# Splitting loaded weights with one instruction of 1024 columns per engine instead of two of 512, with two buffers per part instead of four

## The chip, the cores and the metric

One core of one Trainium2 chip runs the kernel. The metric is device time in microseconds, from the program's start to its end; the shown times are medians of several executions.

## What is computed

One step of a hybrid decoder layer, in float32, for 320 tokens: a prompt of 256 and 8 sequences of 8. The same weights serve all tokens.

```python
proj = rms_norm(x, ln1_g) @ w_in          # 2048 -> 7440 columns
o_a, ... = gdn_mixer(proj[..., :4112])    # gated delta rule, 8 heads of 128
o_b, ... = rwkv_mixer(proj[..., 4112:])   # RWKV-7, 16 heads of 64
x = x + concat([o_a, o_b]) @ w_o          # 2048 x 2048
f, ... = conv_ffn(rms_norm(x, ln2_g))     # w_up 2048 x 11264, conv, silu gate, w_down 5632 x 2048
y = rms_norm(x + f, final_g)              # and the new states of both mixers and the convolutions
```

## The kernel before

Every big product runs as a stream of weights past tokens that stay in SBUF. Weights come from DRAM in pieces of up to 1024 columns (8 tiles of 128x128, 512 KB) into three `raw` buffers of [128, 1024]. To keep float32 accuracy with the fast fp32r matmul, each weight W is split into whi, W rounded to fp32r, and wlo = W - whi. The tokens are split in the same way into xh and xl. For each weight tile, TensorE then does three matmuls of 128x128 by 128x320: whi with xh, whi with xl, and wlo with xh. In a trace, `mm`, `rA`, `rB` and `g` are PSUM tiles that take such sums, and `h`, `fx`, `b`, `bi` hold split tokens.

The split is done in halves. `wpieces` (line 534) cuts all weights into pieces (`self.raws`) and each piece into two parts (`self.halves`): 1024 columns become 512 and 512, and the last piece of a down-projection output, 768 columns, becomes 384 and 384. Three threads feed the stream:

- `wload` (line 553) takes a raw buffer and issues the load on the SyncE queue (line 507).
- `whi` (line 560) takes a buffer of `hi_s` and copies one half with ScalarE (line 438).
- `wlo` (line 567) takes a buffer of `lo_s` and subtracts with VectorE (line 461). When the last half of a piece is done, it frees the raw buffer.

`stream` (line 579) issues the matmuls (line 409) and, when a half has been used up, frees its buffer of `hi_s` and of `lo_s`. Both pools hold four buffers of [128, 512] (lines 670 and 671).

The order of all instructions is made by a planner while the program is built. Work is written as threads that yield operations. `run` (line 339) keeps a modelled clock for each engine and gives out the next operation by readiness and by priority, where a lower number goes first. Each engine then executes its list strictly in that order, so an instruction that waits holds up all behind it on its engine. The stream has priority 1000 on TensorE, and matmuls of the mixers go ahead of it; the mixers' threads have 10 and more, the evacuation of PSUM has 2. A split has priority 1 when it is urgent and 500 otherwise:

```python
urgent = lambda: 1 if self.nsplit - self.np < CFG["ug"] else 500   # line 692; ug is 1
```

Here `nsplit` is the number of the last part whose wlo was given out and `np` the number of the part that the stream is using.

The stages follow each other in one stream: w_ab and w_in (117 pieces, with the mixers' own small operations beside them; `xt`, `bi`, `c`, `s`, `st` are tiles of theirs, and the solve of a triangular system runs on `xt`), w_o in three parts a, b and c (32 pieces), then twice half of w_up (88 pieces) and half of w_down (48 pieces). In part c of w_o each of 16 outputs is half a piece; VectorE adds the sum to x and makes the low part of the next stage's tokens, and GpSimd sums squares (`ssa`).

Of the kernel before, what the change touches and what calls it, by code (L numbers as in the profile page):

```python
# [26 lines left out]
RC = 5  # L27
# [66 lines left out]

CFG = dict(es=0, eg=1, ln=1, bl=0, re=(7,), rg=1, gp={3: 5}, nw=(3, 4), b5=4, b4=4, b2=6, c2=9, b1=12, bi=8, raw=7, xt=2, ord='R0 R1 G0 R2 R3 Z0 G1 R4 R5 Z1 G2 R6 R7 Z2 G3 Z3', dl=1900, wr=2, l2=300, ra=3, war=1, vt=150, lw=1, lh=2, s1=9, st=6, m=60, ev=80, sp=0, cv=0, pq=1000, ug=1, sg=0, gv=1023, fs=105, pl=3000, pd=1000, pr=0.4605, ch=100, gs=1.0, hw=3400, ha=0.42, vg=350, pq2=0, lk=1, mv=126, oc=0, qn=0, aw=1.0, ls=1500, lr=600, lg=1500, hv=114, hs=125, lx=0, l3=3, hp=0, ab=0)

# [71 lines left out]
class Prog:  # L170
# [363 lines left out]
    def wpieces(self, units):  # L534
        self.halves, self.raws = [], []
        for ap, ncol, m in units:
            step = max(m, 1024 // m * m)
            n = -(-ncol // step)
            k = ncol // m
            per = -(-k // n) * m  # L540
            at = 0
            while at < ncol:
                w = min(per, ncol - at)
                self.raws.append((ap[:, at:at + w], w))
                mid = -(-w // m // 2) * m
                for o, z in ((0, mid), (mid, w - mid)):
                    if z:
                        self.halves.append((len(self.raws) - 1, o, z, m, o + z == w))
                at += w
        self.raw, self.hi, self.hl = {}, {}, {}  # L550
        self.nsplit = self.np = self.pk = 0
# [73 lines left out]
    def build(self):  # L625
        tc, a = self.tc, self.a
# [4 lines left out]
        wp = left.enter_context(tc.tile_pool(name="wp", bufs=1))  # L631
        hp = left.enter_context(tc.tile_pool(name="hp", bufs=1))
# [12 lines left out]
        for x in CFG["ord"].split():  # L645
            n = int(x[1:])
# [20 lines left out]
        self.wpieces(units)  # L667
        self.pool_q = [q for q in range(15, 400) if q % CFG["pq"] == CFG["pq"] - 1 and self.halves[q][0] < 2 * 59 + 1]
        self.raw_s = Slots(self, wp, "raw", [P, 1024], CFG["nw"][0])
        self.hi_s = Slots(self, wp, "whi", [P, 512], CFG["nw"][1], F32R)  # L670
        self.lo_s = Slots(self, wp, "wlo", [P, 512], CFG["nw"][1], F32R)
        self.hslots = Slots(self, hp, "h", [P, NTOK], 32, F32R)
        self.gps = PSlots(self, self.ps, "g", [P, 512], 2)
        self.rA = PSlots(self, self.ps, "rA", [P, 512], 2)
# [28 lines left out]
    def start(self):  # L703

        a, V, G, KT = self.a, self.V, self.G, self.KT
        yield self.ms(G, self.ones, 1.0)
        yield self.ms(G, self.eps1, 1e-6)
        if CFG["lk"]:
            yield self.ms(G, self.zero, 0.0)
        yield self.dma(self.vec[:, 0:48], a["vec"][:, 0:48])  # L710
        self.rs = self.b1.take()
        self.h, self.hr, self.hw = {}, {}, {}
        big = [(self.b5, 4)] * 4 + [(self.b4, 3)] * 4 + [(self.b1, 1)] * 4
# [41 lines left out]
        g = yield from self.take(self.gps, 1)  # L755
# [364 lines left out]
    def rwkv(self, i, box):  # L1120
        V, G = self.V, self.G
        b1, b2, b5, gps, s1 = self.b1, self.b2, self.b5, self.gps, self.s1
# [107 lines left out]
        for c0, n in ((0, 2), (2, 2), (4, 1)):  # L1230
            yield from self.want(gps)
            g = gps.take()
            for c in range(n):
                for h in range(2):
                    o = g[:, 256 * c:256 * c + 256].rearrange("p (x h t) -> p x h t", x=2, h=2)[:, :, h]
                    yield self.mm(o, kbc[:, c0 + c], ar[:, c0 + c, :, h])
            m = self.c("rmask" if c0 < 4 else "rmasks")
            m = m.rearrange("p (x t) -> p x t", x=2)
            yield self.tt(V, at[:, c0:c0 + n], g[:, 0:256 * n].rearrange("p (c x t) -> p c x t", c=n, x=2),
                    m.unsqueeze(1).to_broadcast([P, n, 2, P]), ALU.mult)  # L1240
            gps.give()
        scr = self.drams([NS, 1024], f"scr{i}")
        scx = self.drams([8, GG, NS, 32], f"scx{i}")
        sv = scr.rearrange("(f m) (s t) -> f s m t", f=2, t=32)
# [46 lines left out]
            sqd.append(c)  # L1291
        e = G if i in CFG["re"] else V
        st = {"left": 2, "held": ((self.st, dec), (b5, ar_, at_), (b2, kt_, vu_, xd_))}
        sample = self.rwkv_sample(i, st, at, ar, kt, vu, vu_, xd_, xh, yv, dec, sm)
        if CFG["es"] == 2:
            self.spawn(sample, self.cur.prio + CFG["sp"])
        yield from self.solve(mt_, xt_, tm_)
# [146 lines left out]
                    m[:, j:j + 1, j + 1:32].to_broadcast([np_, q, w]), ALU.mult)  # L1444
            yield self.tt(V, x[:, 0:q, j + 1:32], x[:, 0:q, j + 1:32], t, ALU.subtract)

    def rwkv_sample(self, i, st, at, ar, kt, vu, vu_, xd_, xh, yv, dec, sm):
        V, G = self.V, self.G
        ident = self.c("ident")[0:64, 0:64]
        yield from self.want(self.b4)  # L1450
        w_ = self.b4.take()
        ss = w_[:, 0:512].rearrange("p (b x) -> p b x", b=NB)
        yield self.dma(ss, self.a["srw"][i], lag=CFG["ls"])
        yield self.ms(G, w_[64:128, 512:768], 0.0)
# [23 lines left out]
        yield from self.want(self.b4)
        vm_ = self.b4.take()
        vm = vm_[:, :].rearrange("p (h b x) -> p h b x", h=2, b=NB)  # L1480
        for h in range(2):
            yield self.tt((self.g(4), V)[h], vm[:, h], vu[:, 4, h:h + 1].to_broadcast([P, NB, 64]),
                    self.c("bm").unsqueeze(2).to_broadcast([P, NB, 64]), ALU.mult)
# [4 lines left out]
        yield from self.want(self.rB)
        pb = self.rB.take()
        for h in range(2):  # L1490
            yield self.mm(pb[64 * h:64 * h + 64], kt[:, 4, 64 * h:64 * h + 64], vm_[:, 512 * h:512 * h + 512])
        yield self.tt(V, w_[:, 0:512], w_[:, 0:512], pb, ALU.add)
        self.rB.give()
# [401 lines left out]
    def gdn_sample(self, p, st, kq, kw, vn, xd, qkd, ob, ssk, hd):  # L1895
        V, G = self.V, self.G
        gs, b4, s1 = self.gs, self.b4, self.s1
        yield from self.want(b4, 4 if CFG["eg"] == 0 else 3)
        ss = [b4.take(), b4.take()]
        rp_ = b4.take()  # L1900
        kr, rr = (rp_[:, o:o + 512].bitcast(F32R).rearrange("p (g x) -> p g x", g=4) for o in (0, 512))
# [11 lines left out]
        yield from self.want(s1, 1)  # L1913
        hi = s1.take()[:, :].bitcast(F32R)
        yield from self.triple(kr, kw[:, 4], hi, 1)
        yield from self.want(self.rA, 1, s1, 2)
        pa = self.rA.take()
        rt, qs = s1.take(), s1.take()
# [8 lines left out]
        yield lambda: "x" in st  # L1927
        yield self.mm(pa[:, 256:384], xd[:, 4], rt)
        yield self.pcp(rt, pa[:, 256:384], 4)
        yield self.mm(pa[:, 384:512], qkd[:, 4], rt)  # L1930
        yield self.tt(V, ob[:, 4], pa[:, 384:512], qs, ALU.add)
        self.spawn(self.gdn_square(ob, ssk, 4, hd), self.cur.prio)
        self.rA.give()
        if not CFG["gv"] & 1:
            for h in range(2):
                yield self.tt(G, sv[h], sv[h], gs["gls"][:, p, h].unsqueeze(2).to_broadcast([P, NB, P]), ALU.mult)
        yield from self.triple(rr, rt, hi, 0)
        s1.give(3)
        kr = rp_[:, 0:512].bitcast(F32R).rearrange("p (h q x) -> p h q x", h=2, q=2)
# [141 lines left out]
```

## Time and profile before

| what | value |
|---|---|
| median of 3 runs | 1716.24 us (1713.74 to 1716.97) |
| the profiled execution | 1717.03 us, span 1715.2 us |
| TensorE busy | 1677.3 us, 98% of the span |
| VectorE busy | 1239.8 us, 72% |
| ScalarE busy | 1021.7 us, 60% |
| GpSimd busy | 178.7 us, 10% |
| moved by DMA | 256.53 MB, mean 150 GB/s |

The span goes from the first to the last instruction; the execution's time has some 1.8 us more. In the profile PE is TensorE's matmul, PEld its weight load, DVE is VectorE, ACT ScalarE, POOL GpSimd. L409 is line 409. A row of a timeline merges equal instructions that follow each other ("x2") and ends with the idle time of the engine before them, and what ended it.

### The profile page before, as it was taken

To read this page: it belongs to the slowest core of one execution; us is meant where nothing else is said; L and a number is where in the kernel's file an instruction comes from. 1 tells how busy PE (TensorE), PEld (TensorE's weight loads), DVE (VectorE), ACT (ScalarE), POOL (GpSimd) and SP (SyncE) were. 2 spreads that over 40 slices of the span, in tenths; PEclk is the share of its full clock that TensorE was granted. 3 is DMA by queue.
4 is the path that set the end of the run, shared out by engine and by line. 5 is a ranking of instruction groups with operands and counts; after the bars stand their busy time and mean duration, and the time that the engine had idled before them with its cause. 6 is when DMAs were issued, how large, how long until landed. Compare 5 with 4: busy or idle time off the path is not lost.

```text
span 1715.2 us, 33329 instructions
## 1 busy us (share of the span) xinstructions
PE 1677.3 (98%) x11959; PEld 1623.2 (95%) x11959; DVE 1239.8 (72%) x3351; ACT 1021.7 (60%) x2394; POOL 178.7 (10%) x482
## 2 busy tenths in 40 slices
PE   8999999999999989999999999999999999999997
PEld 7998999889988989899999999999999999999996
DVE  8989889879998987787666666544466666665443
ACT  7886877688678856666555544433345545545442
POOL 0200000000000000231111111000011111110101
PEclk9999999999999999999999999999999999999998
DMA  6444534435353556455444444555444444444544
GB/s 231 130 133 127 170 119 141 124 122 163 114 165 100 171 167 190 138 170 163 153 150 149 148 149 151 147 153 148 152 153 151 151 148 148 150 152 144 154 145 148
DMA packets 102967, 256.53 MB, mean 150 GB/s; under 512 B 31953, under 2 KB 41425, under 8 KB 102801
## 3 DMA queue, kind: packets, MB, share of 16 engines
q1 hardware_dynamic: 102080, 253.09, 47.2%
q8 instruction: 94, 1.54, 0.4%
q10 hardware_dynamic: 720, 1.31, 0.2%
q14 instruction: 73, 0.59, 0.1%
HBM read 239.14 MB, written 15.22 MB: 148 GB/s over the span
## 4 chain that ended last, share of the span: by engine, by line
PE 79%; DVE 7%; DMA 4%; ACT 3%; issue 1%; POOL 0%; SPq 0%; DVEq 0%; ACTq 0%; POOLq 0%
PE mm L409 32%; PE rA L409 22%; PE rB L409 20%; PE g L409 5%; DVE wlo L461 2%; DMA b<-scr 2%; DVE xt L461 1%; ACT b L438 1%; DMA b<-scx 1%; DVE bi L456 1%; DVE b L461 1%; PE g L421 1%; ACT whi L438 0%; ACT L438 0%; DVE h L456 0%
## 5 line engine op out<-in xcount | busy, mean ns | idle before, releaser
L438 ACT ACTIVATE whi<-raw 128x512 fp32r<-128x512 f32 (+2 forms) x842 | 519.6, 621 | 543.2 <-PE mm L409 185.7
L461 DVE TENSOR_TENSOR wlo<-raw,whi 128x512 fp32r<-128x512 f32 (+2 forms) x842 | 573.8, 682 | 336.4 <-ACT whi L438 331.8
L409 PE MATMUL mm<-h,whi 128*128 128x320 f32 x2992 | 689.7, 314 | 0.2 <-DVE h L461 0.2
L409 PEld LDWEIGHTS mm<-h,whi 128*128 128x128 f32 x2992 | 504.3, 189 | 4.1 <-issue 2.2
L409 PE MATMUL mm<-h,wlo 128*128 128x320 f32 x1496 | 470.4, 314 | 0.3 <-DVE wlo L461 0.3
L409 PEld LDWEIGHTS mm<-h,wlo 128*128 128x128 f32 x1496 | 282.2, 189 | 3.6 <-issue 1.3
L409 PE MATMUL rB<-h,whi 128*128 128x320 f32 x1136 | 250.6, 309 | 0.0
L409 PE MATMUL rA<-h,whi 128*128 128x320 f32 x1136 | 250.6, 309 | 0.0
L409 PEld LDWEIGHTS rB<-h,whi 128*128 128x128 f32 x1136 | 189.8, 188 | 0.1
L409 PEld LDWEIGHTS rA<-h,whi 128*128 128x128 f32 x1136 | 189.8, 188 | 0.0
L409 PE MATMUL rB<-h,wlo 128*128 128x320 f32 x568 | 175.6, 309 | 0.3 <-DVE wlo L461 0.3
L409 PE MATMUL rA<-h,wlo 128*128 128x320 f32 x568 | 175.3, 309 | 0.0
L474 POOL COPY sfo<-f 128x18 f32<-128x18 f32 x88 | 61.8, 703 | 690.3 <-DVE f L461 690.3
L409 PEld LDWEIGHTS rB<-h,wlo 128*128 128x128 f32 x568 | 106.5, 188 | 0.7 <-DVE wlo L461 0.6
L409 PEld LDWEIGHTS rA<-h,wlo 128*128 128x128 f32 x568 | 106.5, 188 | 0.0
L456 DVE SCALAR_TENSOR_TENSOR f<-f,vec,f 128x336 f32<-128x336 f32 x176 | 102.9, 584 | 3.6 <-ACT f L438 0.3
L461 DVE TENSOR_TENSOR b<-b,b 80x54 f32<-80x54 f32 (+27 forms) x295 | 76.7, 261 | 9.7 <-ACT b L438 7.0
L409 PE MATMUL rA<-fx,whi 128*128 128x320 f32 x336 | 74.1, 309 | 0.0
L409 PE MATMUL rB<-fx,whi 128*128 128x320 f32 x336 | 74.1, 309 | 0.0
L409 PE MATMUL rA<-b,b 128*32 128x128 f32 (+3 forms) x488 | 55.2, 283 | 2.9 <-DMA b<-srw 2.9
L438 ACT ACTIVATE f<-f,vec 128x336 f32<-128x336 f32 x88 | 50.8, 577 | 10.3 <-DVE f L461 1.5
L409 PEld LDWEIGHTS rA<-fx,whi 128*128 128x128 f32 x336 | 56.1, 188 | 0.0
(261 smaller groups left out, 2356.0 us busy)
## 6 DMA issues: line engine op xcount, KB each, us to landing
raw<-w_up SPq DMA_DIRECT2D x176, 512.0 KB, 3.5
raw<-w_in SPq DMA_DIRECT2D x116, 512.0 KB, 4.0
raw<-w_dn SPq DMA_DIRECT2D x64, 512.0 KB, 3.6
raw<-w_dn SPq DMA_DIRECT2D x32, 384.0 KB, 3.1
raw<-w_oa SPq DMA_DIRECT2D x16, 512.0 KB, 3.9
b<-sgdn SPq DMA_DIRECT2D x8, 512.0 KB, 4.4
o_sgs<-b SPq DMA_DIRECT2D x8, 512.0 KB
raw<-w_ob SPq DMA_DIRECT2D x8, 512.0 KB, 5.2
```

The costliest lines, as they stand in the source:

```text
L409: op = Op("T", cost, (out,), (lhsT, rhs), lambda: self.nc.tensor.matmul(out, lhsT, rhs, start=start, stop=stop))
L421: op = Op("T", (1, 0.836 * self.width(in_), 107), (out,), (in_,), lambda: self.nc.tensor.transpose(out, in_, ident))
L438: lambda: self.nc.scalar.activation(out, in_, func, **kw), {AF.Exp: "E", AF.Ln: "L", AF.Silu: "S", AF.Tanh: "T"}.get(func))
L456: lambda: self.V.scalar_tensor_tensor(out, in0, scalar, in1, op0=op0, op1=op1)))
L461: lambda: e.tensor_tensor(out, in0, in1, op=op)))
L474: return self.shared(Op(self.key(e), v if e is self.V else CFG["gs"] * (120 + 3.33 * n), (out,), (in_,), lambda: e.tensor_copy(out, in_)))
```

## The change

One instruction per engine splits a whole piece. The part that `wpieces` cuts becomes as wide as the piece, so that the second part is empty; the buffers of whi and wlo become [128, 1024], two of each. They take the same space as four of [128, 512]. The diff has further options (`seg`, `ss`, `lz`, `rt`, `pv`, `bw`), among them other ways to compute a part of the mixers; their values keep the old code in use.

```diff
-CFG = dict(es=0, eg=1, ... nw=(3, 4), ... hp=0, ab=0)
+CFG = dict(es=0, eg=1, ... nw=(3, 4), ... hp=0, ab=0, seg=(), ss=0, lz=1000, wf=1, rt=0, pv=0, wn=2, bw=0)
...
     def run(self):
+        turns = list(CFG["seg"])
         while self.threads:
+            while turns and self.clk["T"] >= 1e3 * turns[0][0]:
+                CFG.update(turns.pop(0)[1])
...
                 self.raws.append((ap[:, at:at + w], w))
-                mid = -(-w // m // 2) * m
+                mid = w if CFG["wf"] else -(-w // m // 2) * m
                 for o, z in ((0, mid), (mid, w - mid)):
                     if z:
                         self.halves.append((len(self.raws) - 1, o, z, m, o + z == w))
...
         self.raw_s = Slots(self, wp, "raw", [P, 1024], CFG["nw"][0])
-        self.hi_s = Slots(self, wp, "whi", [P, 512], CFG["nw"][1], F32R)
-        self.lo_s = Slots(self, wp, "wlo", [P, 512], CFG["nw"][1], F32R)
+        ww, wn = (1024, CFG["wn"]) if CFG["wf"] else (512, CFG["nw"][1])
+        self.hi_s = Slots(self, wp, "whi", [P, ww], wn, F32R)
+        self.lo_s = Slots(self, wp, "wlo", [P, ww], wn, F32R)
```

## Rows read from the trace of the kernel before

**Rows 1.** The page, engines: busy us (share of the span) xinstructions

```profile
PE 1677.3 (98%) x11959; PEld 1623.2 (95%) x11959; DVE 1239.8 (72%) x3351; ACT 1021.7 (60%) x2394; POOL 178.7 (10%) x482
```

**Rows 2.** Table of stretches: start:end, length, busy us by engine, clock, DMA

```profile
60.00:600.00 540.00, 529.14 (x4044) 492.81 (x4043) 480.50 (x1747) 425.68 (x1255) 46.76 (x129) 1.00 0.44 137
...
600.00:760.00 160.00, 152.20 (x1155) 141.59 (x1154) 123.39 (x395) 94.81 (x272) 21.24 (x51) 0.98 0.58 172
...
800.00:1700.00 900.00, 900.00 (x6139) 899.84 (x6138) 546.40 (x1026) 425.66 (x724) 91.95 (x269) 1.00 0.48 149
```

**Rows 3.** TensorE's waits: who waited for whom, us in total, times, longest us

```profile
PE mm L409 <- ACT b L438: 5.6, 2, 5.5
...
PE rA L409 <- DMA b<-srw: 2.9, 1, 2.9
...
PE mm L409 <- DVE wlo L461: 0.3, 1, 0.3
```

**Rows 4.** Groups by form: operation, tiles, shape, count, busy us, mean ns, idle

```profile
L438 ACT ACTIVATE whi<-raw 128x512 fp32r<-128x512 f32 x776 | 485.5, 630 | 485.6 <-PE mm L409 171.3 <-PE rB L409 129.1 <-PE rA L409 117.8
...
L438 ACT ACTIVATE whi<-raw 128x384 fp32r<-128x384 f32 x64 | 33.6, 525 | 56.6 <-PE rB L409 22.7 <-PE rA L409 19.4 <-PE mm L409 14.4
...
L461 DVE TENSOR_TENSOR wlo<-raw,whi 128x512 fp32r<-128x512 f32 x776 | 537.5, 694 | 267.8 <-ACT whi L438 263.2 <-DMA o_srp<-s 0.8
...
L461 DVE TENSOR_TENSOR wlo<-raw,whi 128x384 fp32r<-128x384 f32 x64 | 35.8, 559 | 65.3 <-ACT whi L438 65.3
```

**Rows 5.** Timeline of 900 to 912 us: start, duration, engine, operation, [idle before]

```profile
906.34 0.31 PE L409 MATMUL mm<-h,wlo 128*128 128x320 f32 x1
...
906.60 0.63 ACT L438 ACTIVATE whi<-raw 128x512 fp32r<-128x512 f32 x1 [1.14 <-PE mm L409]
...
907.27 0.69 DVE L461 TENSOR_TENSOR wlo<-raw,whi 128x512 fp32r<-128x512 f32 x1
...
907.95 1.21 DVE L456 SCALAR_TENSOR_TENSOR f<-f,vec,f 128x336 f32<-128x336 f32 x2
...
910.16 0.19 PEld L409 LDWEIGHTS mm<-h,wlo 128*128 128x128 f32 x1
...
907.34 0.58 ACT L438 ACTIVATE f<-f,vec 128x336 f32<-128x336 f32 x1
```

**Rows 6.** Chain that ended last: start, us, what, number of instructions

```profile
1121.34 19.35 PE mm L409 x132
```

**Rows 7.** Timeline of VectorE and GpSimd, 747 to 756 us

```profile
753.60 0.54 DVE L456 SCALAR_TENSOR_TENSOR h<-h,vec,h 128x320 fp32r<-128x320 f32 x1
...
754.06 0.47 DVE L461 TENSOR_TENSOR h<-h,mm 128x320 f32<-128x320 f32 x1
...
754.46 0.97 DVE L461 TENSOR_TENSOR wlo<-raw,whi 128x512 fp32r<-128x512 f32 x1
...
755.36 0.54 DVE L456 SCALAR_TENSOR_TENSOR h<-h,vec,h 128x320 fp32r<-128x320 f32 x1
...
753.88 1.01 POOL L461 TENSOR_TENSOR ssa<-ssa,f 128x320 f32<-128x320 f32 x1 [0.75 <-ACT f L438]
```

**Rows 8.** Timeline of ScalarE, VectorE and TensorE, 128 to 138 us

```profile
129.28 1.15 ACT L438 ACTIVATE whi<-raw 128x512 fp32r<-128x512 f32 x2 [0.32 <-DMA raw<-w_in]
...
134.17 0.68 DVE L461 TENSOR_TENSOR wlo<-raw,whi 128x512 fp32r<-128x512 f32 x1
...
134.77 0.22 DVE L461 TENSOR_TENSOR xt<-xt,b 80x66 f32<-80x66 f32 x1
...
137.23 0.57 PE L421 MATMUL g<-cst,bi 128*128 128x128 f32 x3 [1.07 <-DVE bi L456]
```

**Rows 9.** Group of wlo in the stretch of 60 to 760 us

```profile
L461 DVE TENSOR_TENSOR wlo<-raw,whi 128x512 fp32r<-128x512 f32 x266 | 183.0, 690 | 24.1 <-ACT whi L438 22.4 <-DMA o_srp<-s 0.8
```

**Rows 10.** Table of stretches of 5 us, two with a lowered clock

```profile
330.00:335.00 5.00, 5.00 (x27) 4.87 (x26) 3.02 (x13) 3.84 (x11) 0.00 (x0) 0.66 0.67 228
...
625.00:630.00 5.00, 5.00 (x23) 5.00 (x23) 3.20 (x18) 2.15 (x10) 0.00 (x0) 0.50 0.13 12
```

More of the change, by code (lines that the diff above doesn't have):

```diff
@@ L91 @@
 WO = {"a": (8, 9, 10, 11, 12, 13, 0, 1), "b": (2, 3, 4, 5), "c": (14, 15, 6, 7)}
-CFG = dict(es=0, eg=1, ln=1, bl=0, re=(7,), rg=1, gp={3: 5}, nw=(3, 4), b5=4, b4=4, b2=6, c2=9, b1=12, bi=8, raw=7, xt=2, ord='R0 R1 G0 R2 R3 Z0 G1 R4 R5 Z1 G2 R6 R7 Z2 G3 Z3', dl=1900, wr=2, l2=300, ra=3, war=1, vt=150, lw=1, lh=2, s1=9, st=6, m=60, ev=80, sp=0, cv=0, pq=1000, ug=1, sg=0, gv=1023, fs=105, pl=3000, pd=1000, pr=0.4605, ch=100, gs=1.0, hw=3400, ha=0.42, vg=350, pq2=0, lk=1, mv=126, oc=0, qn=0, aw=1.0, ls=1500, lr=600, lg=1500, hv=114, hs=125, lx=0, l3=3, hp=0, ab=0)
+CFG = dict(es=0, eg=1, ln=1, bl=0, re=(7,), rg=1, gp={3: 5}, nw=(3, 4), b5=4, b4=4, b2=6, c2=9, b1=12, bi=8, raw=7, xt=2, ord='R0 R1 G0 R2 R3 Z0 G1 R4 R5 Z1 G2 R6 R7 Z2 G3 Z3', dl=1900, wr=2, l2=300, ra=3, war=1, vt=150, lw=1, lh=2, s1=9, st=6, m=60, ev=80, sp=0, cv=0, pq=1000, ug=1, sg=0, gv=1023, fs=105, pl=3000, pd=1000, pr=0.4605, ch=100, gs=1.0, hw=3400, ha=0.42, vg=350, pq2=0, lk=1, mv=126, oc=0, qn=0, aw=1.0, ls=1500, lr=600, lg=1500, hv=114, hs=125, lx=0, l3=3, hp=0, ab=0, seg=(), ss=0, lz=1000, wf=1, rt=0, pv=0, wn=2, bw=0)
 LAT = {"VV": 127, "AA": 143, "GG": 102, "TT": 0, "VT": CFG["vt"], "AT": CFG["vt"] + 15, "GT": CFG["vt"] + 30, "TV": 196, "TA": 268, "TG": 200,
@@ L709, in start @@
             yield self.ms(G, self.zero, 0.0)
-        yield self.dma(self.vec[:, 0:48], a["vec"][:, 0:48])
+        yield self.dma(self.vec[:, 0:48], a["vec"][:, 0:48], self.A if CFG["pv"] else None)
         self.rs = self.b1.take()
@@ L1229, in rwkv @@
         kbc = kb_[:, :].rearrange("p (c x) -> p c x", c=RC)
[L1230 to L1233, printed above, removed]
-                for h in range(2):
[L1235 to L1241, printed above, removed]
+        if CFG["rt"]:
+            for c0, n in ((0, 4), (4, 1)):
+                yield from self.want(gps, 2)
+                two_ = (gps.take(), gps.take())
+                for c in range(n):
+                    for h in range(2):
+                        z = slice(64 * h, 64 * h + 64)
+                        yield self.mm(two_[h][:, 128 * c:128 * c + 128].rearrange("p (x t) -> p x t", x=2), kb[z, c0 + c].rearrange("p x t -> p (x t)"), ar[z, c0 + c, :, h])
+                m = self.c("rmask" if c0 < 4 else "rmasks")
+                m = m.rearrange("p (x h t) -> p h x t", x=2, h=2)
+                for h in range(2):
+                    yield self.tt(V, at_[:, :].rearrange("p (x c h t) -> p h c x t", c=RC, x=2, h=2)[:, h, c0:c0 + n], two_[h][:, 0:128 * n].rearrange("p (c x t) -> p c x t", c=n, x=2),
+                            m[:, h].unsqueeze(1).to_broadcast([P, n, 2, 64]), ALU.mult)
+                gps.give(2)
+        else:
+            for c0, n in ((0, 2), (2, 2), (4, 1)):
+                yield from self.want(gps)
+                g = gps.take()
+                for c in range(n):
+                    for h in range(2):
+                        o = g[:, 256 * c:256 * c + 256].rearrange("p (x h t) -> p x h t", x=2, h=2)[:, :, h]
+                        yield self.mm(o, kbc[:, c0 + c], ar[:, c0 + c, :, h])
+                m = self.c("rmask" if c0 < 4 else "rmasks")
+                m = m.rearrange("p (x t) -> p x t", x=2)
+                yield self.tt(V, at[:, c0:c0 + n], g[:, 0:256 * n].rearrange("p (c x t) -> p c x t", c=n, x=2),
+                        m.unsqueeze(1).to_broadcast([P, n, 2, P]), ALU.mult)
+                gps.give()
@@ L1293, in rwkv @@
         st = {"left": 2, "held": ((self.st, dec), (b5, ar_, at_), (b2, kt_, vu_, xd_))}
-        sample = self.rwkv_sample(i, st, at, ar, kt, vu, vu_, xd_, xh, yv, dec, sm)
+        sample = self.rwkv_sample(i, st, at, ar, kt_, kt, vu, vu_, xd_, xh, yv, dec, sm)
         if CFG["es"] == 2:
@@ L1445, in solve, with rwkv_sample @@
             yield self.tt(V, x[:, 0:q, j + 1:32], x[:, 0:q, j + 1:32], t, ALU.subtract)
-    def rwkv_sample(self, i, st, at, ar, kt, vu, vu_, xd_, xh, yv, dec, sm):
+    def rwkv_sample(self, i, st, at, ar, kt_, kt, vu, vu_, xd_, xh, yv, dec, sm):
         V, G = self.V, self.G
         ident = self.c("ident")[0:64, 0:64]
-        yield from self.want(self.b4)
+        yield from self.want(self.b4, 1 + CFG["bw"])
         w_ = self.b4.take()
+        vm_ = self.b4.take() if CFG["bw"] else None
         ss = w_[:, 0:512].rearrange("p (b x) -> p b x", b=NB)
@@ L1477, in rwkv_sample @@
         self.s1.give(rr)
[L1478 to L1483, printed above, removed]
+        if CFG["ss"] & 1:
+            scs = self.drams([P, 2, P], f"scs{i}")
+            for n, z in enumerate((kt_, vu_)):
+                yield self.dma(scs[:, n], z[:, 512:640], self.q)
         yield self.mm(pa[:, 384:512], at[:, 4, 1], vu_[:, 512:640], start=False)
@@ L1487, in rwkv_sample @@
         self.rA.give()
[L1488 to L1493, printed above, removed]
+        if not CFG["bw"]:
+            yield from self.want(self.b4)
+            vm_ = self.b4.take()
+        if CFG["ss"] & 1:
+            sr = scs.rearrange("(x q s t) w c -> x s t q (w c)", x=2, q=2, s=4)
+            for x in range(4):
+                for n in range(2):
+                    o = 32 * x + 8 * n
+                    yield self.dma(vm_[o:o + 8, 0:512].rearrange("p (q y) -> p q y", q=2), sr[n, x], self.q, lag=CFG["lz"])
+        else:
+            vm = vm_[:, :].rearrange("p (h b x) -> p h b x", h=2, b=NB)
+            for h in range(2):
+                yield self.tt((self.g(4), V)[h], vm[:, h], vu[:, 4, h:h + 1].to_broadcast([P, NB, 64]),
+                        self.c("bm").unsqueeze(2).to_broadcast([P, NB, 64]), ALU.mult)
+        if CFG["ss"] & 1:
+            for x in (0, 2):
+                yield from self.want(self.rA, 1, self.rB)
+                two = (self.rA.take(), self.rB.take())
+                for q in range(2):
+                    for h in range(2):
+                        for y in range(2):
+                            z, o = vm_[32 * (x + y):32 * (x + y) + 16], 256 * q + 64 * h
+                            yield self.mm(two[y][64 * h:64 * h + 64, 64 * q:64 * q + 64], z[:, o:o + 64], z[:, o + 128:o + 192])
+                for y in range(2):
+                    sb = ss.rearrange("p (q s) x -> p s q x", q=2)[:, x + y]
+                    yield self.tt(V, sb, sb, two[y][:, 0:128].rearrange("p (q x) -> p q x", q=2), ALU.add)
+                self.rA.give()
+                self.rB.give()
+        else:
+            yield from self.want(self.rB)
+            pb = self.rB.take()
+            for h in range(2):
+                yield self.mm(pb[64 * h:64 * h + 64], kt[:, 4, 64 * h:64 * h + 64], vm_[:, 512 * h:512 * h + 512])
+            yield self.tt(V, w_[:, 0:512], w_[:, 0:512], pb, ALU.add)
+            self.rB.give()
         self.b4.give(vm_)
@@ L1897, in gdn_sample @@
         gs, b4, s1 = self.gs, self.b4, self.s1
-        yield from self.want(b4, 4 if CFG["eg"] == 0 else 3)
+        strips = CFG["ss"] & 2
+        yield from self.want(b4, 4 if CFG["eg"] == 0 else 2 if strips else 3)
         ss = [b4.take(), b4.take()]
-        rp_ = b4.take()
-        kr, rr = (rp_[:, o:o + 512].bitcast(F32R).rearrange("p (g x) -> p g x", g=4) for o in (0, 512))
+        if not strips:
+            rp_ = b4.take()
+            kr, rr = (rp_[:, o:o + 512].bitcast(F32R).rearrange("p (g x) -> p g x", g=4) for o in (0, 512))
         sv = [t[:, :].rearrange("p (b x) -> p b x", b=NB) for t in ss]
@@ L1912, in gdn_sample @@
                 yield self.cp((V, G)[x], dst, kq[h][:, 4, x].rearrange("p (g j t) -> p g j t", g=2, t=8))
-        yield from self.want(s1, 1)
-        hi = s1.take()[:, :].bitcast(F32R)
-        yield from self.triple(kr, kw[:, 4], hi, 1)
+        if not strips:
+            yield from self.want(s1, 1)
+            hi = s1.take()[:, :].bitcast(F32R)
+            yield from self.triple(kr, kw[:, 4], hi, 1)
+        else:
+            scs = self.drams([P, 2, P], f"gscs{p}")
+            sr = scs.rearrange("(a s t) w c -> s t a (w c)", a=4, s=4)
+            yield self.dma(scs[:, 0], kw[:, 4], self.q)
         yield from self.want(self.rA, 1, s1, 2)
@@ L1929, in gdn_sample @@
         yield self.pcp(rt, pa[:, 256:384], 4)
+        if strips:
+            yield self.dma(scs[:, 1], rt, self.q)
         yield self.mm(pa[:, 384:512], qkd[:, 4], rt)
@@ L1936, in gdn_sample @@
                 yield self.tt(G, sv[h], sv[h], gs["gls"][:, p, h].unsqueeze(2).to_broadcast([P, NB, P]), ALU.mult)
+        if strips:
+            s1.give(2)
+            b4.give(km_)
+            yield from self.want(b4)
+            z_ = b4.take()
+            for x in range(4):
+                yield self.dma(z_[32 * x:32 * x + 8, :].rearrange("p (a y) -> p a y", a=4), sr[x], self.q, lag=CFG["lz"])
+            for x in (0, 2):
+                yield from self.want(self.rA, 1, self.rB)
+                pb = (self.rA.take(), self.rB.take())
+                for a in range(4):
+                    for y in range(2):
+                        z = z_[32 * (x + y):32 * (x + y) + 8, 256 * a:256 * a + 256]
+                        yield self.mm(pb[y][:, 128 * a:128 * a + 128], z[:, 0:128], z[:, 128:256])
+                for a in range(4):
+                    for y in range(2):
+                        h, b = a // 2, 4 * (a % 2) + x + y
+                        yield self.stt(sv[h][:, b], sv[h][:, b], gs["gls"][:, p, h, b:b + 1], pb[y][:, 128 * a:128 * a + 128])
+                self.rA.give()
+                self.rB.give()
+            for h in range(2):
+                yield self.dma(self.a["o_sgs"][2 * p + h], sv[h])
+            b4.give(3)
+            self.release(st)
+            return
         yield from self.triple(rr, rt, hi, 0)
```

## The prediction

> **What bounds the kernel now.** The page's engine table comes first: TensorE is busy 1677.3 us, 98% of the span [rows 1]. A mean over stages hides which of them waits, so the table of stretches is next [rows 2]. From 800 to 1700 us (the feed-forward part) TensorE is busy 900.00 of 900 us, with VectorE at 546.40 and ScalarE at 425.66. Nothing but its own matmuls bounds it there; no saving elsewhere can shorten these 900 us, only a new wait can lengthen them. From 60 to 760 us (the mixers) TensorE is idle 10.9 + 7.8 = 18.7 us, while VectorE is busy 480.5 of 540 and then 123.4 of 160: TensorE and VectorE are both nearly full. Third view: what TensorE waits for [rows 3]. Its longest waits end on ScalarE's and a DMA's chain work for the mixers; on the split weights (wlo) it waits 0.3 us in all by that row. So today the split costs TensorE nothing, and the question is whether that stays so with half as many, larger instructions and buffers.
>
> **How much reserve the split has now.** A matmul of 320 columns follows the one before in 19.35/132 = 0.1466 us [rows 6]; a half piece (4 key tiles, 3 matmuls each) lasts 1.76 us on TensorE, a whole one 3.52 us. In the feed-forward part one half goes like this [rows 5]: its buffer's last matmul starts at 906.34, ScalarE starts whi at 906.60 (0.26 later) for 0.63, VectorE starts wlo at 907.27 (0.04 after ScalarE's end) for 0.69. The half is ready 0.26 + 0.63 + 0.04 + 0.69 = 1.62 us after that matmul. With four buffers three halves lie ahead: 36 matmuls, 5.28 us. The first matmul to read wlo is the third of its half, 0.44 us after the last matmul of the half before, and its weight load stands 0.14 ahead, so the due time is 5.28 + 0.30 = 5.58. Reserve: 3.96 us.
>
> **The change, step by step.** Of the new options in the diff only wf=1 and wn=2 do anything; the others are off.
>
> *The instructions.* The trace has no split of 1024 columns. The 384- and 512-column forms give the slope [rows 4]: ScalarE 525 and 630 ns, so 1024 columns take 630 + 4 x 105 = 1.05 us; VectorE 559 and 694 ns, so 694 + 4 x 135 = 1.23 us. Upper ends are two of the old (1.26 and 1.39 us: no saving). An end below the slope would need columns to become cheaper with width, which these rows give no reason for. I take 1.05 and 1.23. What is saved per piece is less than the difference of durations, because instructions that follow each other overlap: two whi together take 1.15 us, 0.52 from start to start, and after a wlo of 0.68 the next VectorE instruction starts at 134.77, 0.60 after 134.17 [rows 8]. On a full VectorE the saving is 2 x 0.60 - (0.60 + 0.54) = 0.06 us a piece; apart from other work it is 2 x 0.694 - 1.23 = 0.16. From 60 to 760 us 266 halves, 133 pieces, are split [rows 9]: 8 to 21 us of VectorE's 604.
>
> *The buffers, feed-forward part.* A buffer is freed when a whole piece has been used, and its successor is due after one other piece. Ready: 0.26 + 1.05 + 0.04 + 1.23 = 2.58 us (2.95 at the upper ends). Due: 3.52 + 0.30 = 3.82 (the load at 910.16 less the matmul at 906.34 [rows 5]). The reserve falls from 3.96 to 1.24 us (0.87). What can stand in front: on ScalarE one instruction of up to 0.58, on VectorE one of the pair of 1.21 us [rows 5], some 0.6; together 1.2, just covered. The planner also helps: a split is urgent (priority 1) when no piece lies ready beyond the one in use, and with two buffers that is so every time one comes free. I cost the 900 us at zero. If the cover goes, each 0.1 us a piece costs 26 us (900/3.52 = 256 pieces).
>
> *Down projection.* Each output has pieces of 1024, 1024 and 768 columns. The first piece of an output is split while the 768 one (18 matmuls, 2.64 us) runs: due at 2.94, ready at 2.58 (2.95), reserve 0.36 (zero). VectorE's add for the output before comes at another turn, when the 768 piece ends and the due time is again 3.82. Zero, with an upper end of 32 outputs x 0.5 = 16 us if an add (0.48 us [rows 7]) gets in front.
>
> *Output projection's last part.* Here VectorE is exactly full: per half an add (0.40 from start to start), a wlo of 0.97 that GpSimd's sum (1.01 us beside it) stretches from 0.69 (0.90 to the next), and a multiply of 0.46: 1.76 us, the 1.76 of TensorE [rows 7]. For a whole piece after: 2 x 0.86 + 1.14 + two stretches of 0.28 = 3.42 of 3.52. It fits, but ready comes at 2.58 + 0.56 and with one instruction in front at 3.7, against 3.82. Eight pieces: 0 to 4 us; I take 1.
>
> *Mixers.* Four effects. (a) VectorE gets its 8 to 21 us back. (b) A link of a mixer's chain that meets a split waits behind 1.23 in place of 0.69 us; with the saving this about cancels in the queue. (c) Splits now go first whenever a buffer is free, where they used to give way until the next half was missing. (d) The reserve is smaller: an engine held up in its own order by more than 1.24 us now stops the stream, where 3.96 was covered. TensorE's idle there is not for weights: at 137.23 it waits 1.07 us for a VectorE chain result [rows 8], while the wlo of 134.17 had been done for over a microsecond; stream matmuls stand behind the late one in TensorE's order. So (a) can win only part of the 18.7 us: -2 us, ends -9 and 0. (c) and (d): +1, ends 0 and +15. The DMA side moves little: a raw buffer is freed when the whole piece is split, 2.58 in place of 1.62 us after the release, with two further raw pieces (7 us of TensorE) loaded by then.
>
> *Clock.* TensorE ran at the lower of its two levels (1.2 in place of 2.4 GHz) for part of two stretches of the mixers, after it had stood idle: 0.66 granted in 330 to 335 and 0.50 in 625 to 630 us [rows 10]: by these two rows 1.7 + 2.5 = 4.2 us. Another order may lose one or gain one: 0, plus or minus 2.
>
> **Sum.** 0 + 0 + 1 - 2 + 1 + 0 = 0. The profiled execution took 1717.03 us, 1.8 of it outside the span of 1715.2, and lies 0.8 above the median of 1716.24. Forecast for the median: 1716.
>
> **A rule against it.** The rows show ScalarE and VectorE far from full from 800 us on and TensorE without a gap [rows 2]. The Trainium skill (Perfetto Trace Analysis, Optimizing Scalar/DVE Operations) says that larger operations pay where the engine is saturated, and that where these engines are not saturated but make others wait, instructions should be broken up. By that rule the change pays at most in the mixers and is a risk in the long stage; the trace agrees so far that there is no gap there to make worse. It stands as the fifth rival below.
>
> **The rivals.**
> 1. Faster: VectorE's queue decides the mixers' idle time. For: they are 89% and 77% full there and waits end on their chain work. Against: most of the idle time is latency. Half of 18.7 us less 2 us for 1: -8, so 1708 (1702 to 1712).
> 2. Slower: the stream stops in the mixers, effects (c) and (d), in 60 to 800 us. From 3.4/149 = 0.02 us a piece on average it is seen; a stop of 0.4 us at one piece in six costs 149/6 x 0.4 = 10, so 1726 (1720 to 1735).
> 3. Slower by the down projection's tight turn: 4 to 16 us, 1720 to 1732, say 1726.
> 4. No saving at all (two of the old per instruction, 1.26 and 1.39): reserve 0.87, still 1716 to 1719.
> 5. A regular gap in the long stage, if both instructions of the 1.21 pair and 0.58 on ScalarE stand in front: 1.79 - 1.24 = 0.55 on one piece of each of 88 outputs: 48 us, 1764.
>
> **How the numbers follow.** A measurement of this kernel can tell about 0.2%, 3.4 us. Chances: forecast 0.36 (own range 1713 to 1719), rival 1 0.31, rival 2 0.20, rival 3 0.06, rival 4 0.03, rival 5 0.04. Faster 0.31; same 0.36 + 0.03 = 0.39; slower 0.30. The range goes from 1706 (about a quarter of rival 1 below) to 1730 (rival 5 and the tails of 2 and 3 above): 0.18 left out.
>
> **What will show it.** Right: splits of 1.05 and 1.23 us; TensorE 900 of 900 from 800 us on, no idle time ended by wlo; the difference, if any, before 800 us. Wrong: waits of TensorE on wlo or whi above 3 us in all (rivals 2, 3, 5; their place tells which), TensorE's idle time in 60 to 760 below 12 us (rival 1), stretches of the mixers at the lower clock other in number than two.

## The result and the profile after

The changed kernel takes 1726.88 us (median of 8 runs, 1724.10 to 1735.16), the kernel before 1717.23 us beside it (8 runs). The ratio is 1.0063, with a 95% interval of 1.0050 to 1.0075: slower by about 10 us. The profiled execution has a span of 1723.7 us, 8.5 more than before.

First the table of stretches of the changed kernel: start:end and length, busy us of TensorE, its weight loads, VectorE, ScalarE and GpSimd (with counts), granted clock, DMA share, GB/s.

```profile
0.00:60.00 60.00, 51.79 (x336) 45.95 (x337) 50.94 (x105) 43.37 (x78) 3.11 (x9) 1.00 0.63 209
60.00:600.00 540.00, 526.02 (x4005) 487.54 (x4004) 474.36 (x1601) 405.82 (x1142) 42.24 (x122) 1.00 0.44 135
600.00:760.00 160.00, 149.26 (x1140) 138.13 (x1139) 123.12 (x396) 86.96 (x239) 18.43 (x53) 0.98 0.54 160
760.00:800.00 40.00, 40.00 (x273) 39.84 (x272) 31.85 (x49) 29.67 (x48) 16.09 (x22) 1.00 0.51 170
800.00:1700.00 900.00, 900.00 (x6140) 900.00 (x6139) 509.47 (x768) 357.67 (x464) 54.71 (x271) 1.00 0.48 150
```

Held against [rows 2]: from 800 us on TensorE is again busy 900.00 of 900 us, although VectorE and ScalarE have less to do. In the mixers its idle time grows from 10.86 to 540 - 526.02 = 13.98 us and from 7.8 to 10.74. So the loss lies wholly ahead of 800 us. Next comes the split itself, in the groups by form (operation, tiles, shape, count, busy us, mean ns):

```profile
L464 DVE TENSOR_TENSOR wlo<-raw,whi 128x1024 fp32r<-128x1024 f32 x388 | 475.2, 1225 | 258.1 <-ACT whi L441 257.2
L441 ACT ACTIVATE whi<-raw 128x1024 fp32r<-128x1024 f32 x388 | 409.8, 1056 | 493.4 <-issue 275.6 <-PE mm L412 102.0 <-PE rB L412 49.0
```

What was worked out from [rows 4] as 1.23 and 1.05 us is measured as 1.225 and 1.056. One turn of the feed-forward part, in the timelines of the engines (start, duration, engine, operation, idle time before):

```profile
900.70 0.31 PE L412 MATMUL rA<-h,wlo 128*128 128x320 f32 x1
...
900.95 1.06 ACT L441 ACTIVATE whi<-raw 128x1024 fp32r<-128x1024 f32 x1 [2.10 <-issue]
...
902.04 1.23 DVE L464 TENSOR_TENSOR wlo<-raw,whi 128x1024 fp32r<-128x1024 f32 x1 [0.44 <-ACT whi L441]
...
904.52 0.19 PEld L412 LDWEIGHTS rB<-h,wlo 128*128 128x128 f32 x1
```

The buffer's last matmul starts at 900.70, the new piece is ready at 902.04 + 1.23 = 903.27, 2.57 us later; it is due with the weight load at 904.52, 3.82 us later. The reserve is 1.25 us; [rows 5] had led to 1.24.

In the mixers TensorE waits on a split twice, and one of the two stops is its longest there (who waited for whom, us in total, times, longest):

```profile
PE g L412 <- DVE wlo L464: 4.2, 1, 4.2
PE mm L412 <- DVE wlo L464: 1.5, 1, 1.5
```

The longest stands near 628 us. The timelines of VectorE, TensorE and SyncE's queue there:

```profile
622.45 1.21 DVE L464 TENSOR_TENSOR wlo<-raw,whi 128x1024 fp32r<-128x1024 f32 x1
628.80 0.49 DVE L464 TENSOR_TENSOR h<-h,mm 128x320 f32<-128x320 f32 x1 [5.15 <-DMA h<-xT]
...
631.45 1.21 DVE L464 TENSOR_TENSOR wlo<-raw,whi 128x1024 fp32r<-128x1024 f32 x1
...
632.72 0.42 PE L412 MATMUL g<-h,wlo 128*128 128x320 f32 x1 [4.24 <-DVE wlo L464]
...
621.74 0.65 SPq L510 DMA_DIRECT2D b<-gscr  x1
622.48 0.40 SPq L510 DMA_DIRECT2D h<-xT  x1
```

VectorE stands 5.15 us before an add that needs a load; the next wlo is behind that add in VectorE's order, and TensorE, which needs it, stops for 4.24 us. In the kernel before a hold-up of VectorE of similar length, here behind ScalarE, cost almost nothing. Its timeline of VectorE has

```profile
101.06 0.55 DVE L456 SCALAR_TENSOR_TENSOR b<-bi,vec,b 128x320 f32<-128x320 f32 x1 [4.28 <-ACT b L438]
```

TensorE's only gap beside it is one of 0.18 us that ended on another result. So the first theory was this: **theory 1**, the smaller reserve lets hold-ups through. The rivals are **theory 2**, splits that always go first delay the mixers' chains, and **theory 3**, any new order of the instructions gives another time, by chance. A fourth, **theory 4**, came with the experiments: the wide instruction itself delays the chains.

**A part of the diff that the prediction missed.** With `bw=0` the new code is not the old one. In `rwkv_sample` the two masked products of the sample tokens now come after the matmul and the row sums of the output, and were ahead of them:

```diff
-        yield from self.want(self.b4)
-        vm_ = self.b4.take()
-        vm = vm_[:, :].rearrange("p (h b x) -> p h b x", h=2, b=NB)
-        for h in range(2):
-            yield self.tt((self.g(4), V)[h], vm[:, h], ...)
         yield self.mm(pa[:, 384:512], at[:, 4, 1], vu_[:, 512:640], start=False)
         yield from self.rows(yv[:, 4], pa, 384, sm[:, 4:5])
...
+        if not CFG["bw"]:
+            yield from self.want(self.b4)
+            vm_ = self.b4.take()
...
+            for h in range(2):
+                yield self.tt((self.g(4), V)[h], vm[:, h], ...)
```

The work is the same, its place in the mixers is not. All kernels of the experiments were made from the changed source, with `wf=0` where the text says "old split" or an expectation says "the kernel before": they hold this move too, and the kernel before alone is without it. Comparisons among them are not touched by it. Every ratio to the kernel before contains it, the result's own too, and no run isolates it.

### The profile page after: what moved, and what is told of

It reads as the page before. It is cut to its first block, busy times and chain, and to the rows that moved or that the text cites. A ratio compares the mean times of both kernels' runs of the same rounds, so it can differ in the third digit from the quotient of the medians.

```text
span 1723.7 us, 31955 instructions
## 1 busy us (share of the span) xinstructions
PE 1678.8 (97%) x11959; PEld 1622.3 (94%) x11959; DVE 1198.2 (70%) x2930; ACT 927.7 (54%) x1973; POOL 139.4 (8%) x482
## 4 chain that ended last, share of the span: by engine, by line
PE 78%; DVE 10%; ACT 6%; DMA 3%; issue 2%; SPq 1%; POOL 0%; DVEq 0%; ACTq 0%
PE mm L412 30%; PE rA L412 22%; PE rB L412 22%; PE g L412 4%; DVE wlo L464 3%; ACT b L441 2%; DVE xt L464 2%; ACT whi L441 2%; DVE b L464 1%; DVE bi L459 1%; DVE b L459 1%; ACT L441 1%; SPq L510 1%; DMA b<-scr 1%; DMA gscr<-b 0%
## 5 line engine op out<-in xcount | busy, mean ns | idle before, releaser
L441 ACT ACTIVATE whi<-raw 128x1024 fp32r<-128x1024 f32 (+2 forms) x421 | 437.3, 1039 | 558.8 <-issue 283.8
L464 DVE TENSOR_TENSOR wlo<-raw,whi 128x1024 fp32r<-128x1024 f32 (+2 forms) x421 | 506.3, 1203 | 324.6 <-ACT whi L441 323.7
L464 DVE TENSOR_TENSOR b<-b,b 80x60 f32<-80x60 f32 (+27 forms) x295 | 75.5, 258 | 5.8 <-ACT b L441 2.4
L477 POOL COPY sfo<-f 128x18 f32<-128x18 f32 x88 | 17.5, 199 | 736.8 <-DVE f L464 736.8
L441 ACT ACTIVATE f<-f 128x336 f32<-128x336 f32 x44 | 21.3, 485 | 82.2 <-DVE f L459 82.1
L412 PEld LDWEIGHTS rB<-fx,whi 128*128 128x128 f32 x336 | 56.1, 188 | 0.1
```

Source lines behind the costliest of these rows:

```text
L412: op = Op("T", cost, (out,), (lhsT, rhs), lambda: self.nc.tensor.matmul(out, lhsT, rhs, start=start, stop=stop))
L441: lambda: self.nc.scalar.activation(out, in_, func, **kw), {AF.Exp: "E", AF.Ln: "L", AF.Silu: "S", AF.Tanh: "T"}.get(func))
L464: lambda: e.tensor_tensor(out, in0, in1, op=op)))
L477: return self.shared(Op(self.key(e), v if e is self.V else CFG["gs"] * (120 + 3.33 * n), (out,), (in_,), lambda: e.tensor_copy(out, in_)))
```

## The experiments

All ratios are to the kernel before, run beside each.

**The reserve alone: three buffers of 512.**

```diff
-nw=(3, 4), wf=1
+nw=(3, 3), wf=0
```

> Instructions of 512 columns as in the kernel before, but three buffers for each part in place of four. Reserve of the split: 2 x 1.76 + 0.30 - 1.62 = 2.20 us, between the 3.96 of before and the 1.24 of the changed kernel. Theory 1 (lost reserve: an engine held up in its own order by a DMA for longer than the reserve stops TensorE): 1719 to 1725 us, TensorE idle between 60 and 800 us longer than before's 19 us, with waits on wlo in it. Theory 2 (splits that always go first delay the mixers' chains): with three buffers one part still lies ready when a buffer comes free, so they are not urgent: 1714 to 1719. Theory 3 (any other order of instructions gives another time by chance): no preference, 1710 to 1727.

1732.55 us, ratio 1.0113 (1.0083 to 1.0144): more than theory 1 asked. TensorE's longest waits, and its stretch from 600 to 760 us:

```profile
PE mm L412 <- ACT b L441: 5.6, 2, 5.4
PE mm L412 <- DVE wlo L464: 3.9, 8, 1.1
PE g L412 <- DMA b<-scx: 2.2, 2, 1.8
...
600.00:760.00 160.00, 148.82 (x1095) 135.70 (x1094) 121.00 (x417) 89.48 (x261) 16.91 (x52) 0.95 0.51 156
```

The first wait is in the first 60 us and was there before [rows 3]. Waits on wlo are there, 3.9 us in 8 stops, but they are a part of the 17 us only. Of the 15.1 us by which the span grew (1730.3 for 1715.2), TensorE's idle time is 4.3; the other 10.8 is its busy time (1688.1 for 1677.3), where the clock was granted less: 0.95 from 600 to 760 us, 0.98 before.

**The priority alone: splits always urgent.**

```diff
-ug=1, wf=1
+ug=4, wf=0
```

> The kernel before (512 columns, four buffers), but every split has priority 1, never 500. Theory 1 (lost reserve): the reserve is the old 3.96 us, so 1714 to 1720 us. Theory 2 (splits first): 1722 to 1728 us, most of the loss of the changed kernel. Theory 3: 1710 to 1727.

1750.45 us, ratio 1.0208 (1.0186 to 1.0230): far above even theory 2's range, with the old instructions and the old four buffers. Its stretches of the mixers and TensorE's longest waits:

```profile
60.00:600.00 540.00, 512.66 (x3865) 472.71 (x3864) 465.05 (x1644) 401.28 (x1188) 38.89 (x116) 0.98 0.41 130
600.00:760.00 160.00, 151.29 (x1131) 138.64 (x1131) 130.22 (x468) 102.39 (x305) 17.90 (x56) 0.96 0.51 156
```

```profile
PE mm L412 <- ACT b L441: 6.4, 2, 5.5
PE rA L412 <- DVE st L464: 4.4, 1, 4.4
PE g L412 <- DVE b L492: 4.4, 3, 3.4
PE g L424 <- DVE bi L459: 3.7, 4, 2.5
PE rA L412 <- DVE st L459: 3.6, 1, 3.6
```

TensorE idles 27.34 us from 60 to 600 us, against 10.86 before. From 60 to 800 us none of its waits is for a split: they end on VectorE's and ScalarE's steps of the mixers' chains (the 6.4 us lie in the first 60 us, and the kernel before has 5.6 there). The clock falls as well: by the rounded shares, 0.98 of 540 and 0.96 of 160 us are some 11 + 6 = 17 us of TensorE's work not granted, against 3 before.

**The stop near 628 us, first try.**

```diff
-yield self.dma(x, a["xT"][:, n])
+yield self.dma(x, a["xT"][:, n], lag=4000)
-yield self.dma(lo, self.dmx[k], lag=CFG["ls"])
+yield self.dma(lo, self.dmx[k], lag=4000)
```

> The changed kernel, where the planner counts 4 us more until the tokens' loads for the output projection land (x and the mixers' results), so that what needs them is placed later on VectorE and ScalarE and holds up fewer splits; the same instructions run otherwise. In the changed kernel VectorE stood 5.15 us and ScalarE 5.39 us before such loads near 628 us, and TensorE 4.24 us behind them. Theory 1 (lost reserve): that stop goes or falls below 1.5 us, 1720 to 1725 us. Theory 2 (splits first): the stop's place was chance, 1725 to 1729 us.

1729.89 us, ratio 1.0088 (1.0064 to 1.0111), above both ranges. It settles nothing, because the stop did not go: in the new order VectorE stood 5.65 us before the scratch load ahead of those loads, and TensorE again 4.21 us behind it.

**Wide instructions with a larger reserve: three buffers of 768.**

```diff
-step = max(m, 1024 // m * m)
+step = max(m, 768 // m * m)
-ww, wn = (1024, CFG["wn"])   # wn=2
+ww, wn = (768, CFG["wn"])    # wn=3
```

> One instruction per engine and piece as in the changed kernel, but pieces of 768 columns (loads of 384 KB) and three buffers of 768 for each part. Reserve: 2 x 2.64 + 0.30 - 2.1 = 3.5 us, nearly that of before, with 0.68 times its instructions. Theory 1 (lost reserve): the loss goes, 1712 to 1720 us. Theory 4 (wide instructions delay the mixers' chains, 0.96 us in place of 0.69): most of the loss stays, 1722 us or more.

1737.86 us, ratio 1.0138 (1.0117 to 1.0159), in theory 4's range and far from theory 1's. It speaks against theory 2 as the whole cause as well: with three buffers a split is not urgent each time that one comes free, and the loss is larger than the changed kernel's. But pieces and loads changed with it, and it ran in one order only, so it does not prove theory 4.

**The order's chance: one number of the planner.** Each pair has the old and the new split with the same modelled delay from VectorE to TensorE; below, an order is named by that delay in ns.

```diff
-vt=150
+vt=153   # order 2; 147 is order 3, 156 is order 4
```

> The kernel before with one number of the planner changed that says nothing of the splits: the modelled delay from VectorE to TensorE is 153 ns in place of 150. The operations are the same, only their order is made anew. Theory 3 (the time depends on the order by chance, and the order of before is a good one): 1722 to 1735 us. Theories 1 and 2 (the split's buffers or priority make the loss): 1713 to 1721.

> As the run before, with 147 ns in place of 150. Theory 3: 1722 to 1735 us. Theories 1 and 2: 1713 to 1721.

> The changed kernel (pieces of 1024, two buffers) with 153 ns in place of 150 for the modelled delay from VectorE to TensorE. Theory 3: within the spread of the two runs with the old split, 1715 to 1735 us. Theories 1 and 2: 1723 to 1731, above both of them.

> As the run before, with 147 ns in place of 150. Theory 3: 1715 to 1735 us. Theories 1 and 2: 1723 to 1731.

> The old split (512 columns, four buffers) with 156 ns for the modelled delay from VectorE to TensorE: a fourth order. Theory 3 (chance of the order): 1.000 to 1.010 of the kernel before.

> The changed kernel with 156 ns; to be held against the old split with 156 ns. Theories 1 and 2 (the change itself loses): above it by 0.3% or more, as in the three orders before. Theory 3 alone: above or below it.

| order | old split | new split | difference |
|---|---|---|---|
| 150 | (not run with the moved products) | 1.0063 | |
| 153 | 1.0036 (1.0019 to 1.0053) | 1.0146 (1.0129 to 1.0163) | 1.10% |
| 147 | 1.0080 (1.0055 to 1.0105) | 1.0193 (1.0174 to 1.0212) | 1.13% |
| 156 | 1.0044 (1.0027 to 1.0061) | 1.0164 (1.0147 to 1.0181) | 1.20% |

The old split's 1721.2 us (153) lies between the ranges of the theories, its 1728.2 (147) in theory 3's; the new split's 1739.8 and 1748.5 lie above every range. The order by itself moves the old split by 0.44% and the new one by 1.3%: theory 3 is right that a single pair says little. But in each of the three pairs the new split is slower, by 1.1 to 1.2%, with intervals that don't touch: the loss belongs to the new split. The slowest, order 147, in the tables of stretches, first with the old split, then with the new:

```profile
60.00:600.00 540.00, 525.39 (x3969) 484.43 (x3968) 469.47 (x1682) 412.34 (x1224) 44.32 (x122) 0.99 0.43 134
600.00:760.00 160.00, 153.62 (x1162) 141.65 (x1161) 129.72 (x446) 97.96 (x286) 16.33 (x52) 0.98 0.55 169
...
60.00:600.00 540.00, 521.41 (x3922) 482.38 (x3921) 461.80 (x1567) 395.04 (x1111) 42.27 (x122) 0.98 0.42 132
600.00:760.00 160.00, 148.25 (x1109) 136.30 (x1108) 121.18 (x409) 90.00 (x248) 16.51 (x50) 0.95 0.51 153
```

With the new split TensorE is idle 18.59 + 11.75 us in place of 14.61 + 6.38, and the clock is lower, 0.98 and 0.95 in place of 0.99 and 0.98. From 800 to 1700 us both are busy 900.00. Over the whole span, from old to new split, TensorE's idle time grows by 8, 13 and 15 us at orders 153, 147 and 156 and its busy time, with the same matmuls, by 9, 7 and 10 us.

Theory 1's own sign is not in these pairs. From 60 to 800 us TensorE waits on whi and wlo for 4.1, 6.1 and 1.0 us with the old split and for 1.9, 0 and 6.5 with the new (orders 153, 147, 156). At order 147 the old split has

```profile
PE mm L412 <- DVE wlo L464: 5.5, 4, 3.5
PE mm L412 <- ACT whi L441: 0.6, 2, 0.4
```

and the new one, the changed kernel's slowest order, has no such wait.

**The stop near 628 us, with TensorE's and VectorE's order untouched.**

```diff
-yield self.dma(x, a["xT"][:, n])
+yield self.dma(x, a["xT"][:, n], self.A)
-yield self.dma(lo, self.dmx[k], lag=CFG["ls"])
+yield self.dma(lo, self.dmx[k], self.A, lag=CFG["ls"])
```

> The changed kernel with the same order of all work on TensorE and VectorE; only the loads of x and of the mixers' results for the output projection are issued from ScalarE's queue in place of SyncE's, where they stand behind a load that waits for a scratch write. This takes away what VectorE waited 5.15 us and ScalarE 5.39 us for near 628 us. Theory 1 (lost reserve): TensorE's stop of 4.24 us behind that wait goes or falls under 1 us, 1722 to 1725 us. Theories 2 and 3: no difference, 1725 to 1729 us.

1728.89 us, ratio 1.0076 (1.0057 to 1.0096): no gain, as theories 2 and 3 expected. The stop did go; in its timelines VectorE's add and TensorE's later gap:

```profile
625.18 0.47 DVE L464 TENSOR_TENSOR h<-h,mm 128x320 f32<-128x320 f32 x1
...
646.11 0.69 PE L412 MATMUL g<-b,b 32*32 32x32 f32 x16 [2.10 <-DVE b L492]
```

The add waits for nothing, and TensorE has no gap at 628. But it now waits 2.10 us at 646 for VectorE's step of a mixer's chain, where it had waited 0.87, and 2.07 us at 619 for ScalarE, where it had waited 1.14; the span is 1723.0 us, 0.7 less. So half of the 4.24 us is lost again at two steps of the chains, one ahead of the old stop and one behind it, and TensorE is busy 1.4 us longer. The largest visible stop was not the price of the change.

**Wide splits that give way.**

```diff
-1 if self.nsplit - self.np < CFG["ug"] else 500
+1 if self.nsplit - self.np < CFG["ug"] and self.pk >= 2 else 500
```

> The changed kernel, where a split becomes urgent only when the stream has used two of the eight tiles of its current piece (0.88 us at the stream's pace); until then it gives way to the mixers' work as in the kernel before. Theory 2 (splits that always go first delay the mixers' chains): 1713 to 1720 us, 7 or more below the changed kernel. Theory 1 (lost reserve): the reserve falls further, from 1.24 to 0.36 us at worst, 1727 us or more.

> As the run before, with 153 ns in place of 150 for the modelled delay from VectorE to TensorE; to be held against the changed kernel with 153 ns (1740 us). Theory 2: 1720 to 1733 us. Theory 1: 1740 us or more. Theory 3 (chance of the order alone): either, with no common sign over the three.

> As the run before with 147 ns; to be held against the changed kernel with 147 ns (1749 us). Theory 2: 1725 to 1741 us. Theory 1: 1749 us or more. Theory 3: either.

Ratios 1.0045 (1.0028 to 1.0062), 1.0115 (1.0099 to 1.0130) and 1.0054 (1.0038 to 1.0070), against 1.0063, 1.0146 and 1.0193: -0.18, -0.31 and -1.39%. Only the third is clear of noise, and it was at the order where the changed kernel had been slowest; the intervals of the first overlap, those of the second just touch. The first lies above theory 2's range by 3 us, the second by 2; the third lies below it. All have theory 2's sign, and none has the further loss that theory 1 wanted from a still smaller reserve: theory 1 falls as the main cause. How much of the change's loss theory 2 explains is not shown by them. Stretches of the first and its waits:

```profile
60.00:600.00 540.00, 530.62 (x4036) 490.94 (x4035) 471.14 (x1603) 407.82 (x1144) 43.49 (x122) 1.00 0.43 136
600.00:760.00 160.00, 151.22 (x1137) 139.11 (x1135) 122.57 (x398) 88.55 (x241) 20.23 (x55) 0.97 0.54 166
```

```profile
PE g L412 <- DVE b L492: 4.2, 5, 1.9
PE mm L412 <- DVE wlo L464: 2.9, 5, 1.1
```

TensorE stops for wlo five times, more often than in the changed kernel, but for 2.9 us in all in place of 5.7: the long stop near 628 us is gone here too. From 60 to 600 us, where the waits on wlo are alike (1.3 and 1.5 us), it idles only 9.38 us, less than the changed kernel's 13.98.

**Priority and reserve alone, at two more orders.**

> Old split (512 columns, four buffers), splits always at priority 1, with 153 ns for the modelled delay from VectorE to TensorE; to be held against the old split with 153 ns, 1.0036 of the kernel before. Theory 2 (splits first): 1.012 or more. Theory 1 (lost reserve) and theory 3 (chance): 1.000 to 1.008, as often below the one it is held against as above.

> As the run before with 147 ns, against the old split with 147 ns (1.0080). Theory 2: 1.015 or more. Theories 1 and 3: 1.004 to 1.012.

> Old split with three buffers of 512 for each part and its old priorities, with 153 ns; against the old split with 153 ns (1.0036). Theory 1 (lost reserve): 1.008 or more, as the run with 150 ns showed 1.0113 against 1. Theory 3: the loss of that run was its order, 0.999 to 1.008.

> As the run before with 147 ns, against the old split with 147 ns (1.0080). Theory 1: 1.012 or more. Theory 3: 1.003 to 1.012.

| order | old split | always urgent | three buffers |
|---|---|---|---|
| 153 | 1.0036 | 1.0201 (1.0183 to 1.0219) | 1.0112 (1.0095 to 1.0129) |
| 147 | 1.0080 | 1.0238 (1.0216 to 1.0259) | 1.0124 (1.0109 to 1.0140) |

Splits at the head of the queue cost 1.65 and 1.58%, one buffer less 0.76 and 0.44%. The first is well beyond the 0.44% by which the order alone moved the old split. The second has the same sign at both orders and lies in theory 1's ranges, but is of the size of that spread. And it does not come by theory 1's way: with three buffers TensorE waits on splits for 2.6 and 5.5 us from 60 to 800 us, with four it waited 4.1 and 6.1.

## Why the prediction was wrong

The forecast was no change, 1716 us. The time, 1726.88, is what its second rival gave (slower in the mixers, 1726, chance 0.20). The place is right, and the sign that was named for it came (waits on splits above 3 us: 5.7). That the number fits is luck: the rival counted stops of 0.4 us at one piece in six, some 25 of them, and there are two stops; with the longer one gone the time did not fall.

- **Durations and reserve:** right. 1.056 and 1.225 us for 1.05 and 1.23; 1.25 us for 1.24.
- **Long stage at zero:** right in every run, 900.00 of 900. The fifth rival is out, and so is the third: the down projection lies in these 900 us.
- **Output projection's last part, +1:** no sign of it beyond two gaps of 0.9 us at its start, which wait for tokens and not for a split; from 753 to 800 us TensorE is busy 47.00 of 47.
- **Mixers, effect (a), -2 us:** failed. VectorE did get time back: over the whole span it is busy 1198.2 us in place of 1239.8, some 0.10 us a piece, inside the 0.06 to 0.16 worked out, and from 60 to 600 us 474.36, 6 less. But TensorE's idle time grew there. The Trainium skill (Perfetto Trace Analysis, Optimizing Scalar/DVE Operations) says that larger operations can improve throughput if the engine is saturated. With VectorE at 89% before and 88% after from 60 to 600 us, this case shows no gain in time from it.
- **Mixers, effects (c) and (d), +1 us:** this is the term that failed. It named the place and both causes, and took them as small. At this order TensorE's idle time in the two stretches grew by 6 us, the moved products included; at three other orders the new split costs 1.1 to 1.2%, 19 to 21 us. Shown for (c): priority alone costs 1.6% with old instructions and buffers; when wide splits give way, all three orders come out faster, one of them (1.39%) beyond noise. Measured for (d): 0.4 to 0.8% for a buffer less, with no more waiting on splits. The step read the reserve as protection for TensorE only. By the code it is also the time for which a split can give way: with two buffers there is no such time, and `urgent` is true whenever a buffer is free. That this is how a buffer less costs is argued from the code, not shown. That the planner puts splits first was counted as help in the long stage, and the price of the same rule in the mixers was put near nothing.
- **Clock, 0 plus or minus 2:** the size is right for this order (0.98 from 600 to 760, as before; TensorE's busy time 1.5 us longer), though the clock fell at three places of the mixers (470 to 480, 630 to 640, 715 to 720 us) and not at two. At other orders the term is too narrow: the new split's busy time is 7 to 10 us longer than the old one's.
- **Only wf and wn do anything:** wrong, the masked products moved. The prediction put the rest of the diff at nothing.
- **The spread:** a new order as such was priced only in the clock; it moved the time by up to 0.44% with the old split and 1.3% with the new, against the 0.2% that the prediction took as the least that can be told.

Of the 8.5 us of span, idle time of TensorE accounts for 3.1 + 2.9 from 60 to 760 and 8.21 - 7.03 = 1.2 in the first 60 us; 1.5 is its longer busy time.

Open: what the moved products cost by themselves at order 150, and so how the 0.63% divides between them and the split. All three runs of the old split with the move are slower than the kernel before, by 0.36 to 0.80%; whether by the move or by their orders no run tells, so at order 150 the split's own share may be all of the 0.63% or next to none. At the three other orders the split alone costs 1.1 to 1.2%. How that divides between priority, the buffers and the wide instruction itself (the run with three buffers of 768 hints at a share) is open too. No kernel here beat the kernel before.

## What to carry to other kernels

Buffers ahead of a busy engine are not only cover against late work: they can also be the time for which preparation gives way to a chain that has no slack, so that fewer of them can cost although the saturated engine waits no longer for the prepared data than before. Before resizing buffers, look up which priorities and conditions count them. Where a planner makes the order anew at every edit, compare at several orders; one pair can be off by as much as the effect.

## What the runs showed of the hardware

GpSimd's small copies became faster though nothing of them was changed. The same group of GpSimd in the kernel before and in the changed one:

```profile
L474 POOL COPY sfo<-f 128x18 f32<-128x18 f32 x88 | 61.8, 703 | 690.3 <-DVE f L461 690.3
...
L477 POOL COPY sfo<-f 128x18 f32<-128x18 f32 x88 | 17.5, 199 | 736.8 <-DVE f L464 736.8
```

They took 703 ns on average where a wlo of VectorE ran beside each of the 88, and 199 ns where VectorE ran nothing beside any of them, as at 901.66 us of the changed kernel. In the kernel with pieces of 768, 86 of them met a wlo and took 680 ns on average; the two that met none took 197 and 198 ns.

TensorE's clock fell to the lower of its two levels (1.2 in place of 2.4 GHz) in parts of the mixers after TensorE had idled. With the new split at order 147, for instance, it was busy 1.05 us from 725 to 730 us, and the granted clock from 730 to 735 us was 0.50. From old to new split TensorE's busy time grew by 9, 7 and 10 us at orders 153, 147 and 156, beside 8, 13 and 15 us more of idle time.
